# Fourteen gate tiles of layer 1 ahead of its attention, eight of them in pairs of seven products

## The chip, the cores and the metric

The kernel runs on one NeuronCore of a Trainium2 chip. The metric is the device time of one execution in microseconds; the time before is 2329.55 us, the median of three runs (2329.05 to 2334.3). Lower is better.

## What is computed

One step of a two-layer trunk over 128 prompt tokens and 512 latent tokens, 640 columns in all, model width 2048. All of it is float32. Each layer does:

```
h  = rms_norm(x) * (1 + scale) + shift          # scale, shift, gate from SiLU(cond) @ ada_w
p  = h @ w_in                                   # one projection, columns split between two mixers
y  = [mixer_1(p) * silu(g1), mixer_2(p) * silu(g2)]
x  = x + gate * (y @ w_out)
```

Layer 0 (2048 -> 6656 columns) has banded attention (A) and a short gated convolution (B). Layer 1 (also 6656 columns) has mixer C, differential attention with 4 heads (two maps to a head, values 256 wide), and mixer D, grouped attention with 8 query heads over 2 key heads, dense over all keys. In columns of 128, layer 1's projection has 8 tiles each of C's q, k, v and gate, 8 of D's q, 2 of D's k, 2 of D's v and 8 of D's gate: 52 tiles, 16 of them gates. Gates need only h; they are multiplied with the attention's result at the end.

## The kernel before

**Precision and one tile.** A float32 product is made of three matmuls: each operand is split into a high part (`hi`, `wh`, a copy by ScalarE) and a rest (`lo`, `wl`, a subtraction by VectorE; `split`, L240). A tile of 128 output columns is computed transposed, as 128 partitions x 640 tokens in two PSUM banks of 320 (`pa`, `pb`). With 16 blocks of the inner dimension, two halves of the tokens and three products that is 96 matmuls of 128x320 (`proj_q`, L269 to 278). The weights come as quarters of 256 KB (`load_raw`, L252), four to a tile, and are split when they arrive.

**`run_tiles` (L309).** It takes a list of jobs (column, function). The first three tiles, the leads, are computed together, unit by unit of four blocks of h, while `make_h` still makes h; then one tile at a time. After each quarter it calls `slot` (L301), which advances the work behind finished tiles: `prep` (norms, rotation and splits of one Q, K or V) by a step, `attn` (an attention generator) by a step, and `fill` by a rate. `fill1` is layer 1's part of the modulation vector, computed on VectorE in blocks of 64 products of 128x256 with weights `adaw` (L191 to 230), at `FILL1` = 0.9 steps a slot from slot `FILL1_FROM` = 24.

**Attention.** For a head of C, `diff_gen` (L1297) takes five query blocks, two score calls to a block: scores into `S` (one PSUM buffer of two banks, L716 to 718), maximum on VectorE (L683), scaling (L685), exponent on ScalarE (L690), later transposes (L704), splits into `pth` and `ptl` and the weighted sum (L1332 to 1334). For a pair of D heads, `pair_gen` (L743) does likewise (L765 to 767). When a new Q, K or V is to overwrite the one that a running attention reads, its generator calls `drain(attn)`, which emits all the attention's steps that are left.

**Order.** The calls above give the program order; the framework's scheduler then orders the instructions of each engine by its own estimate of when they are ready, so that steps emitted together are spread between later matmuls. Loads are issued from SP's queue, stores of y, x and the caches from POOL's.

**Layer 1's jobs (L1373 to 1398).** For each of the heads 3, 0, 1, 2 of C: k, q, k, q, v, v and two gate tiles (of the next head; after the last, two of D). Then for each of four pairs of D's q heads: k and v for the first and third pair, q, q, and two gate tiles; the last two are the gate of C's head 3, multiplied late. The attention of a head starts after its second v tile, and of a pair after its second q tile, beside the gate tiles. Gates are kept in SBUF in the tile `y` (two buffers) until the attention multiplies its result into it.

**Output projections (`project_out`, L1098).** Layer 0's does 4 tiles singly and 12 in six pairs; layer 1's 6 and 10. `run_pairs` (L431) computes two tiles from 2 x 2 blocks of the weights (A11 to A22) and of the operand (B11 to B22, halves of the inner dimension and of the tokens) with seven products of half size in place of eight, each with 8 x 3 matmuls of 128x320 (`pq`, L526 to 528). The third to sixth products need sums of the operand's blocks: `forms` (L1045) loads it again from DRAM, in eight steps of four subtractions and a split of 960 columns (`T`), with one (`t1`) put in place of the second token half of h 0 to 7. The sums of the products use the buffer of the rotation tables (`tables`, as `room`) as scratch, so the tables are loaded again afterwards.

Of the kernel before, what the change touches and what calls it, by code (L numbers as in the profile page):

```python
# [20 lines left out]
P = 128  # L21
# [27 lines left out]
FILL1 = 0.9  # L49
FILL1_FROM = 24  # L50
# [3 lines left out]
def trunk_kernel(ctx: ExitStack, tc: tile.TileContext, I: dict, O: dict):  # L54
# [244 lines left out]
    credit = [0.0]  # L299
# [9 lines left out]
    def run_tiles(jobs, w_ap, make_h, fill=None, rate=0.0, ahead=None, order=(0, 1, 2, 3), before=None,  # L309
                  last=None, by_half=False, trans=[], grace=0, cut=None, summed=None, led=None, fill_from=0, lead_in=None):  # L310
# [8 lines left out]
        else:  # L319
            leads, held, lp = list(range(min(3, len(jobs)))), [], None  # L320
# [4 lines left out]
        for ui, (pos, qd, js) in enumerate(units):  # L325
# [67 lines left out]
        if before:  # L393
            settle()
        else:
            n = pending.pop(0)
            begin(jobs[n][1], pps[n])
        for i in range(lead, len(jobs)):
# [3 lines left out]
            for qd in range(4):  # L402
# [8 lines left out]
                slot(fill, rate if t > fill_from else 0.0)  # L411
# [19 lines left out]
    def run_pairs(cols, w_ap, mov, room, begin, part, done, tail):  # L431

# [57 lines left out]
        def after(p, name, ps):  # L490
# [8 lines left out]
            elif name == "P6":  # L499
                V.tensor_sub(u2, ps, q1)  # L500
                V.tensor_sub(u4, st8["n5"], u2)
                if p == len(cols) - 1:
                    part(p, 0, 1, u4)
            elif name == "P7":
# [3 lines left out]
                part(p, 1, 0, u2)  # L508
            elif name == "P4":
                done(p, 1, 0, ps)  # L510
            elif p == len(cols) - 1:
# [308 lines left out]
    xdram = [dram.tile([P, NT], F32, name=f"xd{k}") for k in range(KT)]  # L820
# [224 lines left out]
    def forms():  # L1045
# [52 lines left out]
    def project_out(l, maker, finish, last, tail):  # L1098

        w = W_OUT[l]  # L1100

        def job(n):
            def f(pp):
                res_load(l, n)
                for i in range(2):
                    res_sum(l, n, pp[i], CS[:1] if i == 0 else CS[1:])
                yield
                finish(n)
            return f

        n0 = N_SINGLE[l]
        go_on = run_tiles([(n * P, job(n)) for n in range(3)], w, maker, order=(0, 2, 1, 3))


        quarters = [(n * P, qd) for n in range(3, n0) for qd in range(4)]
# [10 lines left out]
        for n in range(3, n0):  # L1126
# [15 lines left out]
            prep.append(job(n)(pp))  # L1142
            advance(prep, 1)
# [14 lines left out]
        def done(p, t, h, src):  # L1158
# [4 lines left out]
            elif n in seen:  # L1163
# [3 lines left out]
        run_pairs([(n * P, (n + 1) * P) for n in range(n0, KT, 2)], w,  # L1167
                  {"B11": half_of(0, 0), "T1": half_of(0, 1), "B21": half_of(8, 0), "B22": half_of(8, 1),
                   "T2": form_of(0), "T3": form_of(1), "T4": form_of(2)}, room, begin, part, done, tail)
        drain(prep)  # L1170
# [4 lines left out]
    def y0_maker(k):  # L1175
        if k < 4:
            return make_y0(k)
        if k == 8:
# [4 lines left out]
            attn.append(forms())  # L1183
# [48 lines left out]
    x1 = [None] * KT  # L1232

    def x1_tail(name):

        for k in (range(0, 4) if name == "P6" else range(4, 6)):
            x1_back(k, big("w8", bufs=4) if k < 4 else big("sx" if k == 4 else "sf"))
# [7 lines left out]
    def h1_maker(k, hv):  # L1245
        if k == 0 and hv[0][0] == 0:
            for g in range(3):
                t = big(f"T{g}")
                for i in range(3 if g < 2 else 2):
                    x1_back(6 + 3 * g + i, t, i)  # L1250
            for i in (14, 15):
                x1[i] = st["xr", i]
            nc.sync.dma_start(tables, I["k_tables"])
# [7 lines left out]
        for sl, c in toks:  # L1261
            V.scalar_tensor_tensor(out=t[:, sl], in0=x1[k][:, sl], scalar=gsc[1][:, k, c:c + 1],
                                   in1=st["rbc"][:, sl], op0=ALU.mult, op1=ALU.mult)
            A.activation(hi[:, sl], t[:, sl], AF.Identity, bias=mod[1][:, k, c:c + 1])
# [235 lines left out]
```

## Time and profile before

| what | us |
|---|---|
| median of three runs | 2329.55 |
| the profiled execution | 2333.26 |
| its span, first to last instruction | 2331.3 |
| TensorE busy in the span | 2286.6 |
| VectorE busy | 1572.5 |
| ScalarE busy | 929.2 |
| granted TensorE clock, mean | 0.996 |

The profile comes from one execution. Its span is the time from the first to the last instruction; 1.96 us lie around it. The page lists engine totals, the span in 40 slices of some 58 us, the chain of work that ended last, and groups of instructions by source line, with the idle time of the engine ahead of them. Other views of the trace give busy time by stretch, the waits between engines, DMA sizes with the time to landing, and single instructions in order of time. Matmuls are pipelined, so the duration of one is longer than the time from its start to the next one's.

### The profile page before, as it was taken

To read this page: it belongs to the slowest core of one execution; us is meant where nothing else is said; L and a number is where in the kernel's file an instruction comes from. 1 tells how busy PE (TensorE), PEld (TensorE's weight loads), DVE (VectorE), ACT (ScalarE), POOL (GpSimd) and SP (SyncE) were. 2 spreads that over 40 slices of the span, in tenths; PEclk is the share of its full clock that TensorE was granted. 3 is DMA by queue.
4 is the path that set the end of the run, shared out by engine and by line. 5 is a ranking of instruction groups with operands and counts; after the bars stand their busy time and mean duration, and the time that the engine had idled before them with its cause. 6 is when DMAs were issued, how large, how long until landed. Compare 5 with 4: busy or idle time off the path is not lost.

```text
span 2331.3 us, 41439 instructions
## 1 busy us (share of the span) xinstructions
PE 2286.6 (98%) x15988; PEld 2210.0 (95%) x15988; DVE 1572.5 (67%) x3196; ACT 929.2 (40%) x1935; POOL 133.0 (6%) x181
## 2 busy tenths in 40 slices
PE   7999999999999999999999999999999999999999
PEld 5699999999999999999999999999999999999999
DVE  4559886786876663988855755755756754567576
ACT  4235442433422222544554344444334444444343
POOL 1001000000000000000010100101000001000101
PEclk9999999999999999999999999999999999999999
DMA  9984545445355443844431422413423312128642
GB/s 315 354 267 131 162 116 170 139 119 169 116 180 162 151 139 114 277 142 128 160 98 53 135 82 72 143 52 100 118 72 95 104 46 82 46 74 270 181 122 70
DMA packets 390630, 321.96 MB, mean 138 GB/s; under 512 B 18402, under 2 KB 336368, under 8 KB 389920
## 3 DMA queue, kind: packets, MB, share of 16 engines
q1 hardware_dynamic: 382496, 288.98, 40.9%
q0 software_dynamic: 7216, 28.16, 3.3%
q8 instruction: 126, 2.06, 0.4%
q10 hardware_dynamic: 720, 2.16, 0.3%
q14 instruction: 72, 0.59, 0.1%
HBM read 290.79 MB, written 28.44 MB: 137 GB/s over the span
## 4 chain that ended last, share of the span: by engine, by line
PE 88%; DMA 4%; DVE 4%; ACT 2%; issue 1%; POOL 0%; SPq 0%; ACTq 0%; DVEq 0%; POOLq 0%
PE pa L276 10%; PE pb L277 10%; PE pb L276 10%; PE pb L278 10%; PE pa L277 10%; PE pa L278 10%; PE pq L526 4%; PE pq L528 4%; PE pq L527 4%; PE T L704 2%; PE S L716 1%; PE S L718 1%; PE S L717 1%; DMA yin<-yd 1%; PE T L178 1%
## 5 line engine op out<-in xcount | busy, mean ns | idle before, releaser
L241 ACT ACTIVATE wh<-raw 128x512 fp32r<-128x512 f32 (+1 forms) x490 | 303.1, 620 | 794.7 <-PE pb L277 655.3
L242 DVE TENSOR_TENSOR wl<-raw,wh 128x512 fp32r<-128x512 f32 (+1 forms) x490 | 330.8, 676 | 351.3 <-ACT wh L241 326.1
L276 PE MATMUL pa<-h,wh 128*128 128x320 f32 x1760 | 560.6, 319 | 4.5 <-ACT h L241 3.2
L277 PE MATMUL pa<-h,wh 128*128 128x320 f32 x1760 | 547.3, 312 | 1.8 <-DVE h L242 1.8
L278 PE MATMUL pa<-h,wl 128*128 128x320 f32 x1760 | 546.4, 310 | 0.0
L278 PE MATMUL pb<-h,wl 128*128 128x320 f32 x1760 | 545.4, 310 | 0.0
L276 PE MATMUL pb<-h,wh 128*128 128x320 f32 x1760 | 545.0, 310 | 0.0
L277 PE MATMUL pb<-h,wh 128*128 128x320 f32 x1760 | 544.8, 310 | 0.0
L213 DVE SCALAR_TENSOR_TENSOR acc<-adaw,sT,acc 128x512 f32<-128x512 f32 (+1 forms) x600 | 357.4, 639 | 13.1 <-DMA adaw<-in_ada_w 12.4
L276 PEld LDWEIGHTS pa<-h,wh 128*128 128x128 f32 x1760 | 331.9, 189 | 24.0 <-issue 14.7
L277 PEld LDWEIGHTS pa<-h,wh 128*128 128x128 f32 x1760 | 332.6, 189 | 6.3 <-DVE h L242 2.7
L278 PEld LDWEIGHTS pa<-h,wl 128*128 128x128 f32 x1760 | 332.1, 189 | 1.2 <-issue 1.2
L278 PEld LDWEIGHTS pb<-h,wl 128*128 128x128 f32 x1760 | 330.8, 188 | 2.1 <-issue 2.1
L276 PEld LDWEIGHTS pb<-h,wh 128*128 128x128 f32 x1760 | 330.6, 188 | 1.0 <-issue 0.4
L277 PEld LDWEIGHTS pb<-h,wh 128*128 128x128 f32 x1760 | 330.8, 188 | 0.2
L690 ACT ACTIVATE p<-S,nm,rq 128x768 f32<-128x768 f32 (+3 forms) x120 | 101.2, 844 | 114.8 <-DVE nm L685 81.1
L526 PE MATMUL pq<-h,wh 128*128 128x320 f32 x352 | 110.0, 313 | 0.4 <-DVE xr L1083 0.4
L527 PE MATMUL pq<-h,wh 128*128 128x320 f32 x352 | 108.8, 309 | 0.0
L528 PE MATMUL pq<-h,wl 128*128 128x320 f32 x352 | 108.4, 309 | 0.0
L683 DVE TENSOR_REDUCE nm<-S 128x1 f32<-128x768 f32 (+3 forms) x120 | 91.9, 766 | 16.1 <-PE S L718 14.9
L241 ACT ACTIVATE pth<-T 128x512 fp32r<-128x512 f32 (+1 forms) x132 | 65.9, 533 | 71.4 <-PE T L704 71.3
L527 PE MATMUL pq<-T,wh 128*128 128x320 f32 x264 | 81.4, 308 | 0.0
(303 smaller groups left out, 3382.5 us busy)
## 6 DMA issues: line engine op xcount, KB each, us to landing
raw<-in_od_w_in SPq DMA_DIRECT2D x208, 256.0 KB, 2.8
raw<-in_ev_w_in SPq DMA_DIRECT2D x196, 256.0 KB, 3.0
adaw<-in_ada_w SPq DMA_DIRECT2D x192, 256.0 KB, 3.0
ada<-in_ada_w SPq DMA_DIRECT2D x14, 2048.0 KB, 11.0
adaw<-in_ada_w SPq DMA_DIRECT2D x128, 128.0 KB, 2.3
yd<-y POOLq DMA_DIRECT2D x34, 320.0 KB, 2.8
yin<-yd SPq DMA_DIRECT2D x32, 320.0 KB, 4.8
w<-yd SPq DMA_DIRECT2D x32, 320.0 KB, 4.4
```

What stands on the lines that cost most here:

```text
L213: V.scalar_tensor_tensor(out=a, in0=w, scalar=sT[:, kt, c:c + 1], in1=a, op0=ALU.mult, op1=ALU.add)
L241: A.activation(hi, x, AF.Copy)
L242: V.tensor_sub(lo, x, hi)
L276: PE.matmul(ps, wh[:, i, :], hi[:, sl], start=(j == js[0] if alone else (pos == 0 and j == 0)), stop=False)
L277: PE.matmul(ps, wh[:, i, :], lo[:, sl], start=False, stop=False)
L278: PE.matmul(ps, wl[:, i, :], hi[:, sl], start=False, stop=(j == js[1] - 1 if alone else (pos == 3 and j == 3)))
L526: PE.matmul(ps, wh[:, j, :], hi, start=(h == 0 and j == 0), stop=False)
L527: PE.matmul(ps, wh[:, j, :], lo, start=False, stop=False)
L528: PE.matmul(ps, wl[:, j, :], hi, start=False, stop=(h == 1 and j == 3))
L683: V.tensor_reduce(nm, s, axis=AX.X, op=ALU.max, negate=True)
L690: A.activation(p[:, 0:n], s, AF.Exp, scale=rsc, bias=nm, accum_out=l)
L704: PE.transpose(t[:, i * P:(i + 1) * P], p, ident)
```

## The change

1. Fourteen of layer 1's sixteen gate tiles (all but the two of C's head 3) are computed first, ahead of all K, Q and V: six singly (three of them leads) and eight in four pairs with `run_pairs`. The part of `project_out` that does this is now the function `project`, called by both.
2. `forms` takes its source as an argument. For layer 1 it reads a copy of h in DRAM, `hdram`, which `h1_maker` writes from POOL's queue; for that, h is first made as float32 by ScalarE and then split.
3. x comes back in the order in which the units 0, 2, 1, 3 of the leads need it (`BACK`), and the last pair's missing half of h is read from `hdram` and split again (`front_tail`).
4. Each finished gate half is tanh-ed, multiplied and, with its other half, stored to `gdram`; an attention's start loads its two gates back into `y` (`gates_back`).
5. The tables' load, the change of pools and `odd_start` follow after the pairs.
6. Mixer C's heads now have six tiles each; D's pairs have no gates behind them, and attention takes 1.5 steps a slot in the two tiles after the first and the third pair (`brisk`). `run_tiles` starts without leads. The late gate no longer drains the attention. `FILL1` is 1.0 from slot 4.

```diff
-FILL1 = 0.9
-FILL1_FROM = 24
+FILL1 = 1.0
+FILL1_FROM = 4
...
-    def slot(fill=None, rate=0.0):
+    def slot(fill=None, rate=0.0, steps=1.0):
         advance(prep, len(prep))
-        advance(attn, 1)
+        pace[0] += steps
+        while pace[0] >= 1.0:
+            advance(attn, 1)
+            pace[0] -= 1.0
...
-            leads, held, lp = list(range(min(3, len(jobs)))), [], None
+            leads, held, lp = list(range(min(3, len(jobs)) if make_h else 0)), [], None
...
-                if p == len(cols) - 1:
+                if part and p == len(cols) - 1:
                     part(p, 0, 1, u4)
...
                 V.tensor_add(u2, ps, u2)
-                part(p, 1, 0, u2)
+                if part:
+                    part(p, 1, 0, u2)
+            elif name == "P4" and part:
+                done(p, 1, 0, ps)
             elif name == "P4":
-                done(p, 1, 0, ps)
+                V.tensor_add(u2, ps, u2)
+                done(p, 1, 0, u2)
...
         def then():
+            if not banded:
+                gated[i] = gates_back(i)
...
-            if i < 8:
+            if i < 8 and not load:
                 drain(attn)
...
-    def forms():
+    def forms(src):
...
-                nc.sync.dma_start(ts[i], ydram[j + 8 * i])
+                nc.sync.dma_start(ts[i], src[j + 8 * i])
...
+    BACK = (0, 1, 2, 3, 8, 9, 10, 11, 4, 5, 6, 7, 12, 13)
...
+        if k == 12:
+            attn.append(forms(hdram))
...
-            A.activation(hi[:, sl], t[:, sl], AF.Identity, bias=mod[1][:, k, c:c + 1])
-        for sl, c in toks:
-            V.scalar_tensor_tensor(out=lo[:, sl], in0=t[:, sl], scalar=mod[1][:, k, c:c + 1], in1=hi[:, sl],
-                                   op0=ALU.add, op1=ALU.subtract)
-        if k == KT - 1:
-            close("mid")
-            open_pool("odd")
-            odd_start()
+            A.activation(t[:, sl], t[:, sl], AF.Identity, bias=mod[1][:, k, c:c + 1])
+        sl = slice(toks[0][0].start, toks[-1][0].stop)
+        split(hi[:, sl], lo[:, sl], t[:, sl])
+        if sl.stop == NT:
+            nc.gpsimd.dma_start(hdram[k], t)
...
+    FRONT = [i for i in range(KT) if i // 2 != heads[0]]
+    N_FRONT = 6
+
+    def gate_out(n):
+        g = pools["cur"].tile([P, NT], F32, tag="xr", name="g", bufs=3)
+        return lambda t, sl, src: (
+            A.activation(st[t][:, sl], src, AF.Tanh, scale=0.5),
+            V.scalar_tensor_tensor(out=g[:, sl], in0=st[t][:, sl], scalar=1.0, in1=src, op0=ALU.add, op1=ALU.mult),
+            nc.gpsimd.dma_start(gdram[FRONT[n]], g) if (n in half_done) else half_done.add(n))
...
+    def front_tail(name):
+
+        if name == "P6":
+            for g in range(3):
+                t, ks = big("w8", bufs=4), range(3 * g, min(3 * g + 3, 8))
+                for i, k in enumerate(ks):
+                    nc.sync.dma_start(t[:, i * HALF:(i + 1) * HALF], hdram[k][:, HALF:NT])
+                for i, k in enumerate(ks):
+                    hi, lo = hs[k]
+                    split(hi[:, HALF:NT], lo[:, HALF:NT], t[:, i * HALF:(i + 1) * HALF])
+
+    project(I["od_w_in"][0], [(OD["cg"] + i * P) if i < 8 else OD["dg"] + (i - 8) * P for i in FRONT], N_FRONT, h1_maker,
+            front_job, front_begin, None, front_done, front_tail, by_half=True)
+    nc.sync.dma_start(tables, I["k_tables"])
+    close("mid")
+    open_pool("odd")
+    odd_start()
+
+    def gates_back(i):
+        if i not in FRONT:
+            return None
+        t = y_pair(i)
+        for j in range(2):
+            nc.sync.dma_start(t[:, j, :], gdram[i + j])
+        return t
...
-        for j in range(2):
-            nxt_h = heads[n + 1] if n < 3 else None
-            jobs.append((OD["cg"] + nxt_h * 256 + j * P, gate_job(2 * nxt_h + j)) if n < 3 else
-                        (OD["dg"] + j * P, gate_job(8 + j)))
+
+    brisk = set()
...
-        for j in range(2):
-            jobs.append((OD["dg"] + (h + 2 + j) * P, gate_job(10 + h + j)) if n < 3 else
-                        (OD["cg"] + heads[0] * 256 + j * P, late_gate_job(2 * heads[0] + j, True)))
-    run_tiles(jobs, I["od_w_in"][0], h1_maker, fill1, FILL1, by_half=True, fill_from=FILL1_FROM)
+        if n % 2 == 0:
+            brisk |= {len(jobs), len(jobs) + 1}
+    for j in range(2):
+        jobs.append((OD["cg"] + heads[0] * 256 + j * P, late_gate_job(2 * heads[0] + j, True)))
+    run_tiles(jobs, I["od_w_in"][0], None, fill1, FILL1, fill_from=FILL1_FROM,
+              steps=lambda i: 1.5 if i in brisk else 1.0)
```

More of the change, by code (lines that the diff above doesn't have):

```diff
@@ L819, in trunk_kernel @@
     x0dram = [dram.tile([P, 4 * NT + 1], F32, name=f"x0d{g}") for g in range(4)]
-    xdram = [dram.tile([P, NT], F32, name=f"xd{k}") for k in range(KT)]
+    xdram, hdram, gdram = ([dram.tile([P, NT], F32, name=f"{n}{k}") for k in range(KT)] for n in ("xd", "hd", "gd"))
     y = [None] * KT
@@ L1096, in form_of, with project @@
         return lambda j: (T[j][:, 0, i * HALF:(i + 1) * HALF], T[j][:, 1, i * HALF:(i + 1) * HALF])
[L1098 to L1115, printed above, removed]
+    def project(w, cols, n0, maker, job, begin, part, done, tail, **kw):
+        go_on = run_tiles([(cols[n], job(n)) for n in range(3)], w, maker, order=(0, 2, 1, 3), **kw)
+        quarters = [(cols[n], qd) for n in range(3, n0) for qd in range(4)]
         raws, parts = [], []
@@ L1165, in done @@
             seen.add(n)
[L1167 to L1170, printed above, removed]
+        project(W_OUT[l], [n * P for n in range(KT)], n0, maker, job, begin, part, done, tail)
     make_y0 = y_maker(("q0h", "q0l", "q1h", "q1l"), NT)
@@ L1410, in y1_maker @@
             open_pool("fin")
-            attn.append(forms())
+            attn.append(forms(ydram))
         if k % 8 >= 4:
```

57 lines of the change are left out of this document (42 added, 15 removed).

## The prediction

> **What bounds the kernel now.** The page comes first: its engine totals, its slices, its chain.
>
> ```profile
> span 2331.3 us, 41439 instructions
> PE 2286.6 (98%) x15988; PEld 2210.0 (95%) x15988; DVE 1572.5 (67%) x3196; ACT 929.2 (40%) x1935; POOL 133.0 (6%) x181
> ...
> DVE  4559886786876663988855755755756754567576
> ...
> PEclk9999999999999999999999999999999999999999
> ...
> PE 88%; DMA 4%; DVE 4%; ACT 2%; issue 1%; POOL 0%; SPq 0%; ACTq 0%; DVEq 0%; POOLq 0%
> ```
>
> TensorE is busy for 98% of the span at full clock, and 88% of the chain that ended last is its own work. Every other engine has room on average. So a change pays if it takes matmuls out, and costs if it makes TensorE wait. The next view is the busy time by stretch: the front of the first output projection, its six pairs, the start of layer 1, its heads of mixer C, its mixer D, the start of the last projection.
>
> ```profile
> 900.00:980.00 80.00, 76.02 (x509) 74.31 (x507) 57.30 (x102) 37.66 (x58) 2.16 (x4) 1.00 0.72 231
> 980.00:1130.00 150.00, 149.56 (x1021) 149.10 (x1020) 125.56 (x211) 63.68 (x104) 7.31 (x13) 1.00 0.50 147
> 1130.00:1180.00 50.00, 48.21 (x319) 47.26 (x318) 41.87 (x95) 29.31 (x59) 1.72 (x3) 0.97 0.48 153
> 1180.00:1750.00 570.00, 561.46 (x3906) 547.98 (x3906) 353.59 (x794) 236.15 (x563) 49.80 (x63) 1.00 0.30 91
> 1750.00:2105.00 355.00, 354.82 (x2496) 345.40 (x2495) 212.08 (x454) 162.70 (x328) 17.20 (x19) 1.00 0.25 76
> 2105.00:2160.00 55.00, 53.41 (x360) 52.05 (x358) 44.67 (x78) 26.38 (x41) 2.92 (x5) 1.00 0.89 290
> ```
>
> The columns are the stretch, its length, then busy time and count of PE, its weight loads, DVE, ACT and POOL, clock, DMA share and GB/s. Layer 1's input projection with its attention (1130 to 2105) leaves TensorE idle for 1.8 + 8.5 + 0.2 = 10.5 us. The pairs of seven products, which the kernel already uses in its output projections, run without a gap: 1021 matmuls in 149.56 us, 0.1465 us each. (The group rows give a matmul some 0.31 us, but matmuls overlap; 0.1465 is what one more costs.) In the pairs DVE is busy for 84% of the time, and TensorE does not wait.
>
> **The change part by part.** *Matmuls.* A tile of 128 columns takes 16 x 2 x 3 = 96 matmuls; two take 192. A pair takes 7 products of 8 x 3 = 24, so 168. Four pairs save 96 matmuls, and the built program of the changed kernel holds just 96 fewer of these, with all transposes, scores and weighted sums unchanged in number. 96 x 0.1465 = 14.1 us. That is the whole gain; the six single gate tiles only move.
>
> *The front: layer 1's first tiles.* h now goes through one more ACT pass (a copy), and DVE's last pass is a plain subtraction over 640 columns; 16 h are written to DRAM through POOL's queue, and read back for the sums that the products need ("forms"); the 32 sums, 8 splits of 960 columns and the gates are new here.
>
> ```profile
> L1264 ACT ACTIVATE h<-T,mod 128x512 fp32r<-128x512 f32 x12 | 8.6, 719 | 2.0 <-DVE T L1262 2.0
> L241 ACT ACTIVATE h<-yin 128x640 fp32r<-128x640 f32 x32 | 23.1, 733 | 26.5 <-DMA yin<-yd 24.5 <-PE pb L278 1.7
> L242 DVE TENSOR_TENSOR wl<-raw,wh 128x512 fp32r<-128x512 f32 x466 | 321.2, 689 | 339.5 <-ACT wh L241 314.4 <-PE T L555 23.2
> L565 DVE SCALAR_TENSOR_TENSOR y<-gt_t,pa 128x320 f32<-128x320 f32 x15 | 7.3, 484 | 2.4 <-ACT gt_t L564 2.4
> L1262 DVE SCALAR_TENSOR_TENSOR T<-T,gsc,T 128x512 f32<-128x512 f32 x8 | 6.0, 745 | 0.0
> L1262 DVE SCALAR_TENSOR_TENSOR T<-T,gsc,T 128x128 f32<-128x128 f32 x8 | 2.8, 345 | 0.0
> ```
>
> Is there time for the forms? The product that needs the last of them is the third of the first pair. Ahead of it TensorE has 3 tiles together, 3 alone and 2 products: 6 x 96 + 2 x 24 = 624 matmuls, 91.4 us. The first output projection does nearly the same in the stretch 900 to 980 with 57.3 us of DVE. The changed front adds the first pass of 16 h (0.745 + 0.345 each, 17.4 us), two more single tiles (8 splits at 0.689, 5.5 us) and 10 gate halves (4.8 us): 85 us in 91.4. It fits, with 6 us to spare, and I cost it at nothing; if that cover goes, each us beyond 6 is a us of TensorE. The added copy delays the first h once. That is between nothing and 16 x 0.733 = 11.7 us if every copy lay on the path; ACT has 20.7 of 50 us free in 1130 to 1180, which is nearest to nothing, and I take one copy, 0.7 us.
>
> *The pairs in the front* have the same matmul chain as those of 980 to 1130 and less DVE work (gates in place of residuals and squares): no wait.
>
> *Queues.* SP gets the three table loads behind the front's last product, since its scratch lies in their buffer. Behind them wait the weight loads of the next tiles, but in the built order eight such loads go ahead, 8 x 24 x 0.1465 = 28 us of matmuls, against the 7.3 us below. POOL gets 16 + 14 writes, SP 24 + 14 reads; the DMA share in 1130 to 2105 is 0.25 to 0.48. A gate read back is issued when its attention starts, and its first use comes a few calls, over 10 us, later: hidden.
>
> ```profile
> xd<-xr POOLq DMA_DIRECT2D x16, 320.0 KB, 3.6
> w<-yd SPq DMA_DIRECT2D x32, 320.0 KB, 4.4
> tables<-in_k_tables SPq DMA_DIRECT2D x2, 768.0 KB, 7.3
> ```
>
> The 3.6 us above were written through POOL's queue in the stretch where DVE is 84% busy. [...]
>
> *Attention with less beside it.* This is the cost to weigh. Each head of mixer C had eight tiles, now six; a pair of D heads had two gate tiles behind it, now none (but 1.5 steps a slot). An attention step still needs its ten score calls, and the next head's K or Q forces what is left of it out. The scheduler spreads the remains between the next tile's matmuls, so fewer matmuls stand between two calls.
>
> ```profile
> 1405.04 0.34 PE L716 MATMUL S<-k1h,q1h 128*128 128x384 f32 x1
> ...
> 1406.10 0.28 PE L1332 MATMUL T<-vh,pth 128*128 128x256 f32 x1
> ...
> 1408.25 0.31 PE L276 MATMUL pa<-h,wh 128*128 128x320 f32 x1
> ```
>
> Six score matmuls take 1.06 us, 18 weighted-sum ones 2.15 us. With these, and 24 matmuls of a tile at 3.52 us, I add up TensorE's work from each call to the next in both built orders. Before, seven of the eight attentions have 4.4 to 7.1 us between calls; only the last, which the late gate forces out, has six of its nine intervals under 4 us. After, 23 intervals are under 4 us: two to three in each C head, then 3, 4, 5 and 2 in the pairs. What does such an interval cost? The trace has one place: the last attention. The rows give, from first to last score maximum, a C head, the pair beside the modulation sums, an undisturbed pair, and the last.
>
> ```profile
> 1379.79:1429.44 49.65, 49.55 (x348) 48.93 (x347) 30.67 (x70) 21.08 (x46) 2.21 (x4) 1.00 0.17 50
> 1782.67:1834.87 52.20, 52.20 (x375) 51.69 (x375) 50.93 (x125) 22.39 (x43) 0.48 (x1) 1.00 0.40 120
> 1865.51:1916.75 51.24, 51.24 (x364) 50.94 (x363) 30.65 (x62) 21.77 (x42) 0.56 (x1) 1.00 0.16 47
> 2061.04:2098.90 37.86, 37.82 (x263) 36.19 (x262) 27.84 (x57) 17.64 (x35) 1.16 (x2) 1.00 0.14 44
> ```
>
> The work that I add up for them is 49.1, 50.9, 50.2 and 34.9 us. So an undisturbed one takes 1.0 us more than the sum, the last 3.0: 2.0 us for six short intervals, 0.33 each. That the calls are bound by a chain there fits the next rows.
>
> ```profile
> L683 DVE TENSOR_REDUCE nm<-S 128x1 f32<-128x768 f32 x64 | 61.0, 953 | 2.0 <-PE S L718 1.5
> L685 DVE TENSOR_SCALAR nm<-nm,rq 128x1 f32<-128x1 f32 x80 | 16.8, 210 | 2.1
> L690 ACT ACTIVATE p<-S,nm,rq 128x768 f32<-128x768 f32 x64 | 63.6, 993 | 77.4 <-DVE nm L685 72.8 <-PE pa L278 2.3 <-PE T L704 2.2
> ```
>
> The scores have one buffer: matmuls 1.06, maximum 0.95, scaling 0.21 and exponent 0.99 follow one another, 3.2 us and the handing over, so nearly 4 us. 17 more short intervals at 0.33 are 5.6 us. Below, the bound is nothing (the scheduler's matmuls just cover it); above, 1 us each, 17 us: the shortest intervals have only 2.4 to 3 us of work against the chain.
>
> *The modulation sums on DVE* (64 products of 128x256 to a block) start earlier. Two of the four blocks now fall on an attention, where one did (1782.67, DVE 50.93 of 52.20, 1.0 us longer than the undisturbed pair). The new one is the C head 1: its DVE instructions add up to 53.6 us by the group rows; the old place adds up to 60.4 and showed 50.93, so 45.2 against 44.7 of TensorE. I take 0.5 us; bounds 0 and 8.9 (53.6 - 44.7).
>
> *Sum.* -14.1 + 0.7 + 5.6 + 0.5 = -7.3 us. The profiled execution took 2333.26 us, 1.96 more than its span; the median shown is 2329.55. From the median: **2322.2 us**, 0.31% faster.
>
> **The rivals.** *All of it arrives.* The short intervals cost nothing, as TensorE is busy for 37.82 of 37.86 us in the one place of before, and the waits of the C heads shrink a little. -14.1, up to 2 us more: 2315. Against it: that place was 2 us over its sum all the same.
>
> *Given back in K and V.* TensorE's waits in the C heads are these.
>
> ```profile
> PE T L555 <- DVE m L600: 3.1, 5, 1.4
> PE S L716 <- ACT p L690: 1.5, 1, 1.5
> PE T L555 <- DVE k0l L242: 1.4, 2, 0.8
> PE T L555 <- DVE k1l L242: 0.9, 2, 0.8
> ```
>
> They are K's rotation and splits, with DVE behind the order. Now most of the ten K tiles meet an attention that is being forced out. At 0.7 us more for each of ten, the longest wait of the third and fourth row, 7 us: 2329, no change.
>
> *Attention bound by its own chain* (slower). In the 23 short intervals DVE and ACT also serve K, Q and the weight splits; if the chain then takes 5 us a call and not 4, each short interval costs 1.3 us or more, and its neighbours up to 4.6 (some 20) half a us: 23 x 1.3 + 10 = 40 us, less 14: 2355. It turns slower once a short interval costs 0.8 us (17 x 0.8 = 14). For: ten calls need it in all eight attentions. Against: DVE was 74% busy (27.84 of 37.86) in the old place, and TensorE hardly waited.
>
> *Late forms.* If each of the eight forms waits for its own write and read (3.6 + 4.4 us), nothing ahead, they take some 64 us from the last unit of the three tiles on, which starts at 31 us: 95 and 4 for the splits, 8 us past the 91.4. 2330.
>
> *It doesn't do what it says*: the matmuls are gone from the built program, so this can only be that the pairs run slower than 0.1465 us; the row of 980 to 1130 leaves no room for it.
>
> **How the numbers follow.** Forecast as summed 0.49, all arrives 0.17, given back in K and V 0.17, chain-bound 0.12, late forms 0.05. About 0.3%, 7 us, is what a measurement of this kernel can tell from no change: 2322.6 to 2336.5 is the same. The forecast lies at that edge; its case spreads by 4 us to both sides, a little more than half of it below: 0.28 faster, 0.21 same. With the rivals: faster 0.45, same 0.42, slower 0.13. The range goes from all arrives less a us, 2314, to 2335, the near end of the chain-bound case (short intervals at 0.8 us or a little less); 0.1 above and 0.07 below are left out.
>
> **What would show it.** Layer 1 starts with some 83 us of tiles and 98 us of pairs in which TensorE is busy for over 99%; a gap ahead of the first pair's third product means late forms. The attentions, from first to last score maximum, take 43 to 47 us in the C heads (before 49.7) and 37 to 42 in the first three pairs; more is the chain. Waits of K's transposes for DVE above 10 us in sum mean that K gave the gain back. The prediction is wrong if TensorE's idle time between the front and the last projection is under 6 or over 25 us.

## The result, and the profile after

The changed kernel takes 2352.27 us (median of 4 runs, 2348.26 to 2352.79); beside it the kernel before takes 2329.78. The ratio is 1.0089, with a 95% interval of 1.0071 to 1.0106: it is **slower** by 0.9%, some 21 us, where 7 us less were forecast. In the views PE is TensorE, PEld its weight loads, DVE VectorE, ACT ScalarE, POOL GpSimd and SPq the queue that issues the loads. The page of the profiled execution (2352.79 us), engine totals and chain:

```profile
span 2351.0 us, 41582 instructions
PE 2286.0 (97%) x15892; PEld 2198.7 (94%) x15892; DVE 1640.9 (70%) x3308; ACT 969.6 (41%) x2007; POOL 150.8 (6%) x211
...
PE 83%; DVE 6%; DMA 4%; ACT 3%; issue 2%; POOL 1%; SPq 0%; ACTq 0%; POOLq 0%; DVEq 0%
```

The 96 matmuls are gone (15988 to 15892), but TensorE's busy time has not shrunk, and its share of the chain fell from 88% to 83%; DVE, ACT, POOL and issue took it. The busy time by stretch of the changed kernel: the front's six tiles, its pairs, the six tiles from there to the first score, the C heads, mixer D, the start of the last projection.

```profile
1136.30:1222.70 86.40, 85.80 (x578) 85.48 (x578) 72.80 (x136) 54.22 (x105) 11.39 (x21) 0.99 0.75 241
1222.70:1321.50 98.80, 98.80 (x675) 98.60 (x674) 75.10 (x124) 46.68 (x84) 4.31 (x8) 1.00 0.33 102
1321.50:1426.20 104.70, 97.50 (x651) 95.01 (x651) 61.40 (x136) 37.19 (x87) 7.84 (x8) 0.97 0.45 135
1426.20:1830.00 403.80, 392.19 (x2717) 377.89 (x2716) 263.57 (x608) 179.71 (x434) 40.00 (x51) 1.00 0.30 90
1830.00:2130.00 300.00, 292.17 (x2034) 276.79 (x2033) 204.49 (x445) 151.88 (x313) 21.76 (x24) 1.00 0.28 84
2130.00:2216.40 86.40, 84.31 (x564) 81.32 (x565) 58.61 (x107) 36.70 (x62) 7.56 (x12) 1.00 0.80 254
```

The front is full. Between it and the last projection TensorE stands for 7.2 + 11.6 + 7.8 = 26.6 us, more than the 25 us from which the prediction called itself wrong; the start of the last projection adds 2.1. Idle time undercounts the loss: a matmul of a tile is recorded for 0.31 us, and the next one can start 0.1465 us after it, so the first 0.16 us of a wait still count as busy. So I also subtract from each stage the work of TensorE in the built order (by their starts in the trace of the kernel before, 0.1465 us a tile matmul, 0.18 a score, 0.12 a weighted sum, and 0.088 a transpose, an estimate between the 0.08 each of two in a row and the 0.095 each of six). The rest has no meaning by itself, but its growth has:

| stage, us | before: time, work, rest | after: time, work, rest | growth of the rest |
|---|---|---|---|
| start of layer 1 to first score | 99.3, 92.5, 6.8 | front 186.3, 183.3, 3.0; then 104.9, 92.0, 12.9 | +9.1 |
| first to last score | 864.7, 833.5, 31.2 | 702.0, 649.5, 52.4 | +21.2 |
| last score to the end | 233.2, 222.5, 10.7 | 222.8, 209.5, 13.3 | +2.6 |

The work is 14.2 us less. With 0.9 us that layer 1 starts later, -14.2 + 9.1 + 21.2 + 2.6 + 0.9 = +19.6 us, against 19.7 between the spans. Two places carry it: attention, and the way into it. In the kernel before, the whole stretch from the start of layer 1 to the first score had TensorE idle for 1.8 us:

```profile
1134.14:1233.44 99.30, 97.49 (x656) 94.45 (x657) 64.31 (x136) 52.38 (x120) 6.79 (x7) 0.98 0.35 104
```

### The profile page after: what moved, and what is told of

It is laid out like the page before. It is cut to its first block, busy times and chain, and to the rows that moved or that the text cites. A ratio compares the mean times of both kernels' runs of the same rounds, so it can differ in the third digit from the quotient of the medians.

```text
span 2351.0 us, 41582 instructions
## 1 busy us (share of the span) xinstructions
PE 2286.0 (97%) x15892; PEld 2198.7 (94%) x15892; DVE 1640.9 (70%) x3308; ACT 969.6 (41%) x2007; POOL 150.8 (6%) x211
## 3 DMA queue, kind: packets, MB, share of 16 engines
q10 hardware_dynamic: 720, 2.16, 0.3%
## 4 chain that ended last, share of the span: by engine, by line
PE 83%; DVE 6%; DMA 4%; ACT 3%; issue 2%; POOL 1%; SPq 0%; ACTq 0%; POOLq 0%; DVEq 0%
PE pa L276 9%; PE pa L277 9%; PE pb L277 9%; PE pa L278 9%; PE pb L276 9%; PE pb L278 9%; PE pq L534 5%; PE pq L535 5%; PE pq L536 5%; PE T L712 2%; PE S L724 1%; PE S L726 1%; PE S L725 1%; PE T L178 1%; PE T L563 1%
## 5 line engine op out<-in xcount | busy, mean ns | idle before, releaser
L276 PE MATMUL pa<-h,wh 128*128 128x320 f32 x1632 | 518.5, 318 | 5.5 <-ACT h L241 4.1
L277 PE MATMUL pa<-h,wh 128*128 128x320 f32 x1632 | 508.6, 312 | 2.3 <-DVE h L242 2.3
L278 PE MATMUL pa<-h,wl 128*128 128x320 f32 x1632 | 508.4, 312 | 0.0
L278 PE MATMUL pb<-h,wl 128*128 128x320 f32 x1632 | 506.4, 310 | 0.0
L276 PE MATMUL pb<-h,wh 128*128 128x320 f32 x1632 | 506.0, 310 | 0.0
L277 PE MATMUL pb<-h,wh 128*128 128x320 f32 x1632 | 506.0, 310 | 0.0
L213 DVE SCALAR_TENSOR_TENSOR acc<-adaw,sT,acc 128x512 f32<-128x512 f32 (+1 forms) x600 | 358.1, 639 | 14.9 <-DMA adaw<-in_ada_w 14.2
L276 PEld LDWEIGHTS pa<-h,wh 128*128 128x128 f32 x1632 | 307.8, 189 | 25.0 <-issue 14.3
L277 PEld LDWEIGHTS pa<-h,wh 128*128 128x128 f32 x1632 | 308.5, 189 | 7.5 <-DVE h L242 3.8
L276 PEld LDWEIGHTS pb<-h,wh 128*128 128x128 f32 x1632 | 307.0, 188 | 1.1 <-issue 0.6
L277 PEld LDWEIGHTS pb<-h,wh 128*128 128x128 f32 x1632 | 307.0, 188 | 0.9 <-issue 0.8
L534 PE MATMUL pq<-h,wh 128*128 128x320 f32 x480 | 149.6, 312 | 1.0 <-ACT wh L241 1.0
L535 PE MATMUL pq<-h,wh 128*128 128x320 f32 x480 | 148.3, 309 | 0.0
L536 PE MATMUL pq<-h,wl 128*128 128x320 f32 x480 | 148.0, 309 | 0.0
L535 PE MATMUL pq<-T,wh 128*128 128x320 f32 x360 | 111.1, 309 | 0.0
L534 PE MATMUL pq<-T,wh 128*128 128x320 f32 x360 | 111.0, 308 | 0.0
L536 PE MATMUL pq<-T,wl 128*128 128x320 f32 x360 | 111.0, 308 | 0.0
```

The costliest lines, as they stand in the source:

```text
L213: V.scalar_tensor_tensor(out=a, in0=w, scalar=sT[:, kt, c:c + 1], in1=a, op0=ALU.mult, op1=ALU.add)
L276: PE.matmul(ps, wh[:, i, :], hi[:, sl], start=(j == js[0] if alone else (pos == 0 and j == 0)), stop=False)
L277: PE.matmul(ps, wh[:, i, :], lo[:, sl], start=False, stop=False)
L278: PE.matmul(ps, wl[:, i, :], hi[:, sl], start=False, stop=(j == js[1] - 1 if alone else (pos == 3 and j == 3)))
L534: PE.matmul(ps, wh[:, j, :], hi, start=(h == 0 and j == 0), stop=False)
L535: PE.matmul(ps, wh[:, j, :], lo, start=False, stop=False)
```

## The experiments

**Theory 1, thin attention**: with two gate tiles fewer beside each attention, TensorE waits for its chains on DVE, ACT and POOL; some 20 us. **Theory 2, the way into attention**: set-up loads and the modulation sums' early start delay the first K tiles; some 8 us. Rivals: the pairs or forms cost time of their own; the sums' blocks hit attentions; a wait that is taken away only moves to the next instruction in the order. Times on several chips are compared by their ratio to the kernel before on the same chip; 0.001 is 2.3 us.

### The way into attention: e1_con_early, e4_fill_old

In the changed kernel SP's queue and ACT stand here (SP's timeline, ACT's, and SP's waits):

```profile
1323.41 0.46 SPq L1427 DMA_DIRECT2D tables<-in_k_tables  x1
1323.96 0.38 SPq L1290 DMA_DIRECT2D lam<-in_c_lambda  x1
1330.05 0.33 SPq L1302 DMA_DIRECT2D con<-in_c_out_norm  x1
...
1332.96 0.38 SPq L666 DMA_DIRECT2D ctxv<-in_cache_c_v  x1
```

```profile
1338.93 0.63 ACT L241 ACTIVATE vh<-ctxv 128x512 fp32r<-128x512 f32 x1 [6.18 <-DMA ctxv<-in_cache_c_v]
```

```profile
SPq L1302 <- DMA gd<-g: 5.7, 1, 5.7
```

con goes into a buffer that opens when the last gate has been stored; the cached V's load is queued behind con, and ACT, in its order, waits 6.2 us for that V ahead of K's copies and the weight splits.

```
e1  -    nc.sync.dma_start(lam4, ...), ... dma_start(con, ...)   behind the front, buffers of the new pool
    +    the same ahead of the front, buffers of their own
e4  -FILL1 = 1.0; FILL1_FROM = 4
    +FILL1 = 0.9; FILL1_FROM = 24
```

> The changed kernel, with the three small loads that its layer-1 set-up needs (the two of lam and the one of con) issued ahead of the front, in buffers of their own, so that nothing of SP's queue waits for the front's last gate any more. Same work, same order otherwise. Theory 'the way into attention' (of the changed kernel's 20-odd us more than the sum, 6 to 9 come from its first 50 us behind the front: con's load waits 5.7 us on SP for a gate's store, the loads of the cached K and V stand behind it, ACT stands 6.2 us at the first copy of the cached V ahead of K's copies and weight splits): 2343 to 2347 us, and TensorE's idle time from 1321 to 1390 falls from some 10 us to 3 or less. Rival 'thin attention' (TensorE waits for the softmax and output chain of attention in all eight heads, since two gate tiles fewer lie beside each): the eight attentions' excess over their TensorE work stays near 28 us whatever happens here; if it is the whole cause, 2350 to 2353.

> The changed kernel with the modulation sums paced as before (0.9 a slot from slot 24, not 1.0 from slot 4), so that the DVE blocks of 64 products fall later. Theory 'the sums' blocks hit two attentions' (step four of the prediction, priced at 0.5 us with 8.9 as its upper end): 2343 to 2349 us. Rival 'thin attention' with 'the way into attention': within 2 us of the changed kernel, 2350 to 2354, the waits only shifted to other heads.

Measured: e1 2348.18 us, ratio 1.0065 (1.0048 to 1.0083); e4 2345.41 us, 1.0059 (1.0036 to 1.0081). The stretch from the front's last product to the first score, and for e4 a stretch of the last projection as well:

```profile
1319.79:1419.16 99.37, 94.55 (x653) 92.28 (x652) 59.74 (x131) 37.12 (x86) 7.84 (x8) 1.00 0.46 139
```

```profile
1317.34:1412.26 94.92, 94.34 (x653) 92.35 (x652) 39.30 (x78) 37.16 (x87) 7.35 (x8) 1.00 0.37 110
2130.00:2145.00 15.00, 9.81 (x52) 8.14 (x51) 7.77 (x15) 5.59 (x8) 0.00 (x0) 0.77 0.78 258
```

The stretch had 104.89 us in the changed kernel (rest 12.9); early loads make it 99.37 (rest 7.4), later sums 94.92 (rest 2.9) with DVE at 39.3 and not 61.4 us. In the time of the whole kernel e1 gives 4 to 6 us, a little less than it was expected to, and e4 about 7. So Theory 2 holds and the sums are the larger half of it, though not where the prediction had looked: they do not hit attentions (first to last score takes 702.0, 702.5 and 698.9 us in the three), they hit K's rotation on DVE. K's transposes, which TensorE does behind that rotation, waited 6.1 us for DVE in the changed kernel, 4.5 in e1 and not at all in e4. Yet in e4 the queue is as late as before, and ACT still waits for the cached V:

```profile
ACT vh L241 <- DMA ctxv<-in_cache_c_v: 6.0, 1, 6.0
```

TensorE is idle for only 0.6 us there. So the late loads cost much only on top of the early sums. e4 returns part at the end, where sums left over stop TensorE 4.7 us: in its row of 2130 to 2145 TensorE is busy for 9.81 of 15 us, at a granted clock of 0.77.

### Moving gates without pairs: e3_all_single

```
-project(..., N_FRONT, h1_maker, front_job, front_begin, None, front_done, front_tail, by_half=True)
+run_tiles([... all 14 gates as single tiles ...], I["od_w_in"][0], h1_maker, order=(0, 2, 1, 3), by_half=True)
```

> The changed kernel without its four pairs: all fourteen gate tiles ahead of attention are single tiles of 96 matmuls, no form is made and h is not written to DRAM. TensorE's work is 14.1 us more than in the changed kernel (that of the kernel before), everything from attention on is in the same order. Theory 'thin attention' plus 'the way into attention' (moving the gates is the cost, the pairs work as priced): the changed kernel's time plus 13 to 15 us, 2365 to 2368. Rival 'the pairs or the forms cost time of their own' (the front slows, or the forms delay DVE into attention): less than 8 us above the changed kernel, below 2360.

Measured: 2360.15 us, ratio 1.0117 (1.0096 to 1.0138), some 6.5 us over the changed kernel by the ratios, 7 by the profiled spans. That is about the number of the rival, but the profile takes it apart differently. First the front of e3 and its way into attention, then the changed kernel's front:

```profile
1135.37:1334.89 199.52, 199.52 (x1350) 199.23 (x1350) 75.72 (x135) 70.19 (x137) 7.09 (x13) 0.99 0.33 104
1334.89:1431.76 96.87, 94.77 (x653) 92.31 (x652) 60.84 (x135) 37.27 (x87) 7.86 (x8) 1.00 0.45 132
```

```profile
1135.03:1321.32 186.29, 185.69 (x1254) 185.17 (x1254) 148.44 (x262) 100.89 (x189) 15.71 (x29) 0.99 0.53 168
```

The pairs save 199.5 - 186.3 = 13.2 us of the 14.1 priced. The way into attention is 8.0 us shorter in e3 (96.9 against 104.9), and from the first score on both agree within 1.5 us. The pairs and forms cost nothing of their own; their end meets the way into attention worse. In e3, ACT waits 0.3 us for the cached V, where it waited 6.2.

### Attention compressed, and given its tiles back: e2_two_steps, e5_gates_twice

```
e2 (from the kernel before)   -advance(attn, 1)   +for _ in range(2): advance(attn, 1)     in layer 1 only
e5 (from the changed kernel)  +the 14 gate tiles once more, beside attention as before; the front's are not read;
                              no tile goes at 1.5 steps a slot
```

> The kernel before, in which layer 1's attention goes two steps a slot and not one. Not one matmul is added, removed or put into a pair; the gates stay where they were; only the attention's calls stand closer (32 to 35 us of TensorE's work from first to last score maximum by the built order, before 49 to 50; 3.5 to 4.4 us between calls). Theory 'thin attention': this alone costs 15 us or more (2345 to 2365 us), with the waits of TensorE at the output's transposes and at scores. Rival 'the way into attention', or a cost of the pairs, the gates' DRAM round trip or the DVE sums: no more than 3 us change, 2327 to 2333.

> The changed kernel, with its fourteen gates computed a second time as single tiles in their old places beside attention (the products of the front are stored and never read back): fourteen tiles of 96 matmuls more, which is 197.8 us of TensorE's work by the built order, and attention again has the tiles beside it that it had. Theory 'thin attention' (the missing tiles cost 17 to 20 us in the eight attentions): the extra tiles are paid for in part by waits that they fill, so 2352 + 198 - 18 = 2532 us, and attention's excess over TensorE's work falls from 28 to some 10 us. Rival (the waits belong to the front, the way into attention, the queues, or to the order of attention itself): 2550 us or more.

Measured: e2 2348.60 us, ratio 1.0065 (1.0044 to 1.0086), e5 2527.27 us (two executions), 1.0834 (1.0813 to 1.0856). One C head of e2, then e2's waits at the output's transposes in all four heads, then one C head of e5; the heads from first to last score maximum:

```profile
1386.74:1421.35 34.61, 34.06 (x234) 32.37 (x233) 25.58 (x62) 16.79 (x38) 2.22 (x4) 1.00 0.11 33
```

```profile
PE T L1352 <- DVE on L1346: 6.6, 12, 0.6
PEld T L1352 <- DVE on L1346: 6.3, 8, 0.8
```

```profile
1567.85:1617.50 49.65, 49.56 (x348) 48.93 (x347) 30.65 (x69) 21.10 (x46) 2.22 (x4) 1.00 0.18 50
```

Without one matmul moved, closer attention alone costs 15 to 17 us. With the gates back beside attention, 198 us of matmuls cost 175 us (2527 less the changed kernel's 2352; 1.0089 times the kernel before gives 2352 on that chip too), the head is at its old 49.65 us, and the rest from first to last score is 33.5; it was 31.2 before and 52.4 in the changed kernel. The other 4 us or so that e5 wins lie ahead of the first score. Theory 1 is shown as to place and size. In e2 most of the 72 intervals between calls are at 3.5 to 4.7 us, and they cost 16.8 / 72 = 0.23 us each; the changed kernel's 23 short ones would cost 0.92 each. So short intervals between score calls are not what counts.

What is? The time that TensorE lost from first to last score (start to start, over the work of the instructions between), by the instruction that came next (the last four kernels come further below):

| us lost ahead of | before | after | e2 | e5 | e6 | e10 | e7 | e11 |
|---|---|---|---|---|---|---|---|---|
| scores | 2.7 | 6.5 | 8.0 | 0.1 | 6.6 | 8.1 | 7.2 | 8.8 |
| transposes of p | -0.1 | 4.1 | 1.3 | 0.1 | 4.8 | 1.4 | 1.0 | 1.3 |
| weighted sums | 0.4 | 9.0 | 3.6 | 2.9 | 9.0 | 7.0 | 3.5 | 2.4 |
| output's transposes | 3.1 | 10.5 | 8.5 | 2.5 | 8.6 | 6.9 | 12.2 | 1.1 |
| K's transposes | 5.7 | 2.0 | 7.9 | 6.6 | 3.1 | 5.0 | 6.0 | 6.3 |
| tiles and other | 9.0 | 10.2 | 8.8 | 11.9 | 10.3 | 13.8 | 9.8 | 11.5 |
| sum | 20.8 | 42.4 | 38.1 | 24.3 | 42.2 | 42.2 | 39.7 | 31.4 |

Scores took only 3.8 us more; the steps behind them took 20.2 more. Both mixers lose, as the idle time shows: mixer C and mixer D before, then both after, cut at the first score of D.

```profile
1233.44:1781.33 547.89, 541.12 (x3766) 528.68 (x3765) 339.23 (x764) 226.00 (x528) 44.68 (x57) 1.00 0.31 91
1781.33:2098.11 316.78, 316.66 (x2232) 308.97 (x2230) 196.14 (x423) 144.22 (x291) 15.53 (x17) 1.00 0.25 75
```

```profile
1426.21:1872.86 446.65, 433.86 (x3009) 416.85 (x3008) 296.45 (x690) 201.03 (x481) 44.82 (x57) 1.00 0.32 97
1872.86:2128.17 255.31, 249.35 (x1732) 236.91 (x1732) 170.22 (x359) 129.39 (x264) 16.94 (x18) 1.00 0.24 72
```

TensorE's idle time grows from 6.8 to 12.8 us in C and from 0.1 to 6.0 in D. The lost time taken by mixer grows by about 11 us in each: in C mostly ahead of the output's transposes (+8) and the transposes of p (+4), in D ahead of weighted sums (+5) and scores (+4). In the changed kernel's timeline one wait at the output's transposes reads (`on` is the block's output on its way to being normalised):

```profile
1457.79 0.28 PE L1347 MATMUL T<-vh,ptl 128*128 128x256 f32 x1
...
1458.11 0.49 DVE L1349 TENSOR_SCALAR on<-T,rl 128x256 f32<-128x256 f32 x1
1458.49 0.99 ACT L698 ACTIVATE p<-S,nm,rq 128x768 f32<-128x768 f32 x1 [4.17 <-DVE nm L693]
...
1459.48 0.41 ACT L1352 ACTIVATE junk<-on 128x256 f32<-128x256 f32 x1
...
1461.23 0.56 POOL L1355 TENSOR_TENSOR rn<-ssq,half 128x1 f32<-128x1 f32 x1 [6.81 <-DVE ssq L1353]
1461.83 0.49 DVE L1356 SCALAR_TENSOR_TENSOR on<-on,rn,con 128x256 f32<-128x256 f32 x1 [0.69 <-POOL rn L1355]
...
1462.46 0.41 PE L1362 MATMUL T<-ident,on 128*128 128x128 f32 x2 [0.88 <-DVE on L1356]
```

From the last weighted sum to the transposes the block goes through DVE, ACT (behind the exponent of the next scores), DVE, POOL and DVE: 4.4 us, and the order holds work for TensorE for all but 0.9 us of them.

### Both ways in mended, and the output's transposes: e6_con_and_fill, e8_out_later, e10_tail_later

```
e6   e1's edit, and FILL1 = 1.04; FILL1_FROM = 24
e8   e6, and out(u - 2) moved behind score(u, 0), groups(u - 1) and the yield
e10  e8, and     +def finish(): out(3); out(4); save_y(...)
                 +late.append(finish)        run at the start of the next slot
```

> The changed kernel with both edits of the first four runs together: the set-up loads ahead of the front, and the modulation sums from slot 24 on, but at 1.04 a slot, so that none is left over for the end of layer 1 (at 0.9 some 17 of the 132 steps were, and TensorE stood 4.7 us there and ran at half clock behind it). If the two causes add up: TensorE idle for less than 2 us between the front and the first attention, no stall at the end, 2337 to 2341 us. What is left above 2316 is 'thin attention'. If both edits took away the same stall: 2344 to 2346.

> The kernel of the second run of this set, in which the transposes of a C head's finished block come half a step later, behind the next score call, so that the chain ahead of them (scale, square, power on POOL, scale) has one more call's time. Nothing else changes. Theory 'thin attention', with this chain as what TensorE waits for in the C heads (14 waits of 1.0 us at the transposes in the changed kernel): 4 to 8 us below the run without it. If the softmax chain (scores, maximum, exponent in the one score buffer) is the bound instead, the waits only move to the scores: within 2 us of it.

> The changed kernel with the set-up loads early and the modulation sums from slot 24 on (its run: 2341.2 us), in which only the transposes of a C head's finished blocks are moved: half a step later, and those of the last two blocks a quarter of a tile after the attention. By the waits of the kernel without it (7.9 us at these transposes, 3.4 us at the next transposes of p, which wait for the product that empties the same PSUM tile): theory 'forced out against its own chain' 2331 to 2335 us; rival 'the waits only move', as half a step alone showed (2340.4): 2338 to 2342.

Measured: e6 2341.23 us, ratio 1.0040 (1.0025 to 1.0054); e8 2340.38 us, 1.0033 (1.0023 to 1.0043); e10 2338.68 us, 1.0037 (1.0024 to 1.0051). The way into attention of e6, and e10 from first to last score with its waits there:

```profile
1318.61:1412.94 94.33, 94.11 (x653) 92.34 (x652) 38.03 (x73) 37.11 (x86) 7.34 (x8) 1.00 0.36 106
```

```profile
1411.29:2113.14 701.85, 685.94 (x4741) 656.20 (x4739) 486.19 (x1106) 329.44 (x744) 62.54 (x75) 1.00 0.31 93
```

```profile
PEld S L728 <- ACT p L702: 6.3, 17, 0.7
PEld T L1365 <- DVE ptl L242: 6.3, 9, 1.4
```

e6 removes the way into attention (94.33 us, rest 2.3): e1 left a rest of 7.4 and e4 one of 2.9, so the two overlap. What is left of the loss is in attention (rest 52.1, before 31.2). In e10 no transpose waits for `on` any more, and the sum of the table stays at 42.2: the transposes now stand behind the splits of p (ptl), the scores behind the exponent. This form of Theory 1, that the chain behind the weighted sums is the bound, **fell**.

### Cover from the projection's own tiles: e7_third_query, e9_query_and_tail, e11_tail_no_k, e12_tail_and_k

```
e7   e6, and Q's tiles: tag "q", bufs=3   (gates read back: bufs=1)
     -drain(attn)                          +if tag == "q1": drain(attn)
     C heads: q0, k0, q1, k1, v0, v1       (was k0, q0, k1, q1, v0, v1)
     D: q0 k0 q1 v0 | q2 q3 | q4 k1 v1 q5 | q6 q7 | the two late gates
     attention at 1.1 to 1.25 steps a slot in 18 tiles (was 1.5 in four); D's second K no longer drains it
e11  e7 with e10's later transposes
e9   e11, and one more yield ahead of K's transposes
e12  e10, and the same yield (two Q buffers, old order)
```

> The kernel of the run before, and attention gets cover from the projection's own tiles: Q tiles rotate in three buffers and not two (the gates that are read back have one buffer and not two, to make the room), the next head's first Q tile comes ahead of its first K tile and no longer forces attention out, and in mixer D the tiles are put in an order that leaves 8 to 11 tiles' quarters to each pair, where 5 or 6 were. No matmul is added or removed; the built order has 46 to 50 us of TensorE's work from first to last score in the C heads, 40 to 52 in the pairs. Theory 'thin attention': the excess of the eight attentions falls to 10 to 15 us, and the time to 2318 to 2330. Rival: no better than the run before.

> The kernel with three Q buffers, with two more edits. The transposes of a C head's finished blocks come half a step later, and those of its last two blocks are not forced out with the attention but come a quarter of a tile (24 matmuls) after it, since they need neither Q, K nor V; and K's transposes come a quarter of a tile later than they did, behind its rotation on DVE. Waits at the output's transposes were 11.8 us (15 of them) in the kernel with three Q buffers, at K's rotated rows 4.8 us. Theory 'attention is forced out against its own chain' (what costs is not how many matmuls lie beside an attention on average, but that its last steps are issued with nothing between them, so that TensorE stands for the chain behind each): both go, 2321 to 2327 us. Rival 'DVE and ACT have too much to do in this stage' (the waits move to scores and weighted sums): within 4 us of the kernel without it, 2332 to 2340.

> The kernel that was fastest (2325.3 us: three Q buffers and tile order, output transposes later, K's transposes a quarter of a tile later), without the last of the three. Three Q buffers alone gave 5 us (2336.1), the later transposes alone 2.5 (2338.7 against 2341.2), all three 16. If cover and later transposes need each other (each alone only hands the wait to the next link of the chain): 2325 to 2331 us. If K's later transposes are what made the difference: 2333 to 2337.

> The changed kernel with the set-up loads early, the modulation sums from slot 24 on, the output transposes later, and K's transposes a quarter of a tile later, but with the two Q buffers and the tile order that it had. If cover for attention is needed beside the later transposes: 2334 to 2340 us. If K's later transposes do it alone: 2326 to 2331.

| | two Q buffers, old order | three Q buffers, new order |
|---|---|---|
| transposes as they were | e6 2341.23, 1.0040 | e7 2336.12, 1.0023 (1.0013 to 1.0032) |
| output's transposes later | e10 2338.68, 1.0037 | e11 2325.89, 0.9977 (0.9967 to 0.9986) |
| and K's a quarter later | e12 2336.01, 1.0022 (1.0012 to 1.0031) | e9 2325.28, 0.9976 (0.9966 to 0.9986) |

The stretch from first to last score in e7 with its waits there, then in e11:

```profile
1413.21:2104.65 691.44, 670.92 (x4683) 646.38 (x4682) 479.25 (x1099) 326.90 (x737) 64.27 (x75) 1.00 0.31 93
```

```profile
PEld T L1364 <- DVE on L1358: 14.2, 14, 2.0
PE T L1364 <- DVE on L1358: 10.1, 15, 1.7
```

```profile
1412.72:2095.43 682.71, 670.60 (x4684) 648.24 (x4682) 478.50 (x1100) 326.35 (x737) 64.99 (x75) 1.00 0.31 94
```

e7 changes buffers, order and pace at once, and none of these was tried alone; I call them cover together. Cover alone gives 4 to 5 us, which is less than Theory 1 had expected of it (2318 to 2330 us), later transposes alone 2.5 at most, both 15: they need each other. With cover alone the weighted sums stop waiting (9.0 to 3.5 us in the table) and the output's transposes, still forced out with the attention's end, wait more (8.6 to 12.2); with both they wait 1.1. K's later transposes give 0.6 us or less with the cover; without it, from e10 to e12, 2.7 to 3.5 us, though the two intervals overlap and the runs are from different chips. e9 and e11 **beat both kernels**: 0.23 to 0.24% under the one before, with all four pairs. Their rest from first to last score is 39 to 41 us, before 31.2; what holds these last 8 to 10 us was not tried.

## Why the prediction was wrong, step by step

- *Matmuls, -14.1*: right. 96 are gone, and e3's front against the changed one gives 13.2 us.
- *The front, +0.7, and its forms at nothing*: right. Both parts run at 99% or more, as the last part of the prediction asked. The rival "late forms" fell: no gap stands ahead of the first pair's third product, and h's writes, issued from 1140.4 to 1170.3, took 3.6 us with DVE busy for 29.4 of 31 us, the same as xd's writes before:

```profile
hd<-T POOLq DMA_DIRECT2D x16, 320.0 KB, 3.6
1140.00:1171.00 31.00, 30.40 (x207) 30.08 (x207) 29.37 (x56) 27.77 (x56) 8.69 (x16) 1.00 0.79 270
```

- *Queues, "hidden"*: **failed**. The step counted SP's weight loads ahead of the tables and called the rest cover. It left out what else SP issues there: con, whose buffer opens only when the last gate is stored, and behind it the cached K and V, which ACT meets in its order. e4 bounds the harm: with the sums late, the same wait of ACT leaves TensorE idle for only 0.6 us. The gates read back did not matter.
- *The modulation sums, +0.5, bounds 0 and 8.9*: **failed as to place**. It asked which attentions the blocks hit; the early start hit the first K tiles, whose rotation is on DVE. Taken together with the queue this is the +9.1 of the first table; e6 takes 10.6 of the stretch away (104.9 to 94.3).
- *Attention with less beside it, +5.6, bounds 0 and 17*: this is the term that **turned the sign**: +21.2, above its upper bound. That TensorE would wait in attention was right; what was priced was not. It counted intervals from score call to score call, at 0.33 us by the last attention, which is a pair of mixer D. At the scores themselves TensorE lost 3.8 us more. The other 20.2 are at the steps between (transposes of p, weighted sums) and at the output's transposes of the C heads, behind a chain (scale, square, power, scale) that a D pair does not have. But the price was too low for D as well: its pairs lose about 11 us more, where even all 14 of their short intervals at 0.33 make 4.6. One place, with one attention forced out, did not stand for a pair beside other tiles.
- *Given back in K and V*: between first and last score K's transposes lost 3.7 us less, not more. Ahead of the first score they waited 6.1 us, but for the modulation sums and not for an attention that is forced out.
- *Attention bound by its own chain*: this rival came true in kind, and its number (2355 against 2352) partly by luck: it had 40 us for attention, which took 21.2, and nothing for the way into it. Its price of 1.3 us a short interval was for the wrong waits. Its chance of 0.12 rested on "TensorE hardly waited in the old place", a D pair at that.
- *What would show it*: the C heads took 46.5 to 47.4 us and the first three pairs 40.0, 43.3 and 41.1, mostly inside or just over the bounds given (43 to 47, 37 to 42). These bounds were too wide to tell +5 from +20, for a C head's work by the order is only some 44. The bound on TensorE's idle time did tell it.

## What to carry to other kernels

Work that looks like filler beside a latency-bound chain is part of that chain's schedule: before it is moved, price every step of the chain that the filler covers, to its last consumer, in every place that will lose it. When one wait goes, look for the next link before you count the gain: here two edits worth 5 and at most 2.5 us alone were worth 15 together. And when a stage is moved, list all that each queue issues behind it, and what the stage that now comes first needs from DVE.

## What the runs showed of the hardware that was not expected

Behind two waits of TensorE in the changed kernel (3.92 and 2.16 us) the granted clock was 0.56 and 0.58 for some 3 us; behind one of 2.96 us in e1 it was 1.00. In the changed kernel's timeline of TensorE:

```profile
1348.21 0.38 PE L616 MATMUL T<-ident,ctxk 128*128 128x128 f32 x2
1352.52 0.66 PE L563 MATMUL T<-ident,m 128*128 128x128 f32 x4 [3.92 <-DVE m L608]
...
1355.38 0.47 PE L276 MATMUL pa<-h,wh 128*128 128x320 f32 x1
1355.64 0.47 PE L277 MATMUL pa<-h,wh 128*128 128x320 f32 x1
...
1356.91 0.31 PE L276 MATMUL pb<-h,wh 128*128 128x320 f32 x1
1357.06 0.31 PE L277 MATMUL pb<-h,wh 128*128 128x320 f32 x1
...
1386.90 0.66 PE L563 MATMUL T<-ident,m 128*128 128x128 f32 x4 [2.16 <-DVE m L608]
```

and in that of e1:

```profile
1381.05 0.66 PE L563 MATMUL T<-ident,m 128*128 128x128 f32 x4 [2.96 <-DVE m L608]
```

The granted clock is the column before the last two: behind the two waits of the changed kernel, then behind that of e1.

```profile
1353.00:1356.20 3.20, 3.20 (x16) 2.97 (x15) 3.20 (x9) 0.88 (x2) 0.00 (x0) 0.56 0.76 220
1387.00:1390.50 3.50, 3.50 (x17) 3.48 (x18) 3.50 (x10) 0.88 (x2) 0.00 (x0) 0.58 0.66 196
```

```profile
1381.00:1384.00 3.00, 2.81 (x19) 2.56 (x20) 3.00 (x8) 0.92 (x3) 0.00 (x0) 1.00 0.66 184
```

Behind the wait of 3.92 us matmuls start 0.27 us apart for some 3 us at a clock of 0.56, then 0.15 again; the same follows the wait of 2.16 us at 1386.90, at 0.58. A dozen matmuls 0.27 us apart and not 0.15 are some 1.5 us more, by estimate, behind each. Behind e1's wait of 2.96 us they start 0.15 us apart at once, at a clock of 1.00. The length of the wait alone does not tell the three apart, for the one of 2.16 us was followed by the lower clock and the one of 2.96 us was not; what does was not shown.
